# Scaling half of a gate table on ScalarE, and 38 instead of 30 products worked out ahead

## The chip, the cores and the metric

The kernel runs on one core of a Trainium2 chip. The metric is the device time of one execution in microseconds (us), and of several executions the median. The engines are TensorE (PE in the rows; its weight loads are PEld), VectorE (DVE), ScalarE (ACT), GpSimd (POOL, which here issues the gathers of table rows) and SyncE (SP, which issues the other transfers). Each engine works through its own queue in order.

## The reference

One layer of a hybrid decoder runs for 1024 prompt tokens and 8 sample tokens: three mixers (a state-space scan, a convolution branch, attention to a memory), an output projection with layer norm, and then a layer of experts with a second layer norm. The change lies in the expert layer. Each token picks, in each of 8 heads, 16 of 128 x 128 experts, each named by two numbers i and j:

```
u = jnp.take(u_tab, idx, axis=0)
act = jax.nn.gelu(jnp.einsum('td,thkd->thk', t, u), approximate=False)
v = jnp.take(v_tab, idx, axis=0)
return jnp.einsum('thk,thkd->td', gate * act, v)
```

`u_tab` and `v_tab` (here: the first and the second table) have 16384 rows of 1024 numbers.

## The kernel before, in words

The prompt is worked on in three groups of 256, 384 and 384 tokens. For the first two groups the table rows that the tokens chose are gathered one slot at a time: a row of the first table for each of 128 tokens is one gather (L442) of 128 x 1024 numbers, which VectorE multiplies with the tokens and sums (L455). The rows of the second table are either added up on VectorE (L544, `block_v2`) or, in `block_v`, multiplied on TensorE (L501) with a mostly empty weight tile ("slide"); I call eight of these matmuls, which take four gathered tiles, a strip. The sums of a strip block stand in the accumulators named `va` until VectorE reads them (L522). These rows are not a stage of their own. They are spread over the other work: each call of `product` calls `spread`, which lets a number of rows go, set by `PHASES` and `PACE`, with a low priority.

The third group is worked on in full, with no gathers of its own, by `dense_group`. For each of 128 blocks of experts (all j for one i) it needs

- a product: the first table's block times the 384 tokens, followed by Gelu (`activations`, L1296). Ahead of the dense loop it is made with plain fp32 matmuls (L211); in the loop with operands split into a high and a low part (L189 and L191 split the table, L200 multiplies three combinations);
- its gates: for each token the gate at the places (i, j) that the token chose, 0 elsewhere;
- the second table's block, split by L164 and L176 and multiplied in L1385 into six accumulators.

The gate tables are built first, four tokens at a time, in three blocks of 128 tokens: 96 token groups. For each, VectorE compares the token's i with 0 to 127 (L1315, `oi`, four tokens in one instruction), and compares its j with 0 to 127 and scales by the gate (L1319, `oj`, one instruction per token). TensorE multiplies the two (L1321), which puts a token's gates in one of two accumulator banks named `mm`, and ScalarE evicts the bank (L1325) into a tile that goes to memory as `gd`. `oi` and `oj` are taken from a pool of seven tiles (`E2B`). Between the token groups stand products: the first 6 (`PRE`) stay on the chip; then one after every fourth token group (`STEP`) until 30 (`EARLY`) are done, whose results go to memory as `ad`. At the start of each block `route` works out the choices of 128 tokens on VectorE (L343 to L419).

Then the dense loop runs over c from 0 to 127. Iteration c takes product c+6 from `ad` while c+6 is under `EARLY` (and lets rows go at the rates of `PACE[-2]`, 1.0 and 1.0 a call), and computes it afterwards (2.2 and 2.2). VectorE multiplies it with its gates (L1353); I call this a weighing, and there are 128 of them. `keep_tokens`, which copies the group's tokens out, is called at c = 2 x `EARLY`.

A scheduler sets the order on each engine when the program is built: it may move a product past token groups, and puts the gathered rows where it finds room. So a change of a constant moves instructions far from its line.

Of the kernel before, what the change touches and what calls it, by code (L numbers as in the profile page):

```python
# [13 lines left out]
AF = mybir.ActivationFunctionType  # L14
OP = mybir.AluOpType
# [3 lines left out]
P = 128  # L19
# [23 lines left out]
RIDE = 0  # L43
LATER = 1000000
PRE = 6
EARLY = 30
STEP = 4
VLAG = 6
TLAG = 10
E2B = 7  # L50
# [18 lines left out]
def hybrid_layer(ctx: ExitStack, tc, I, O):  # L69
    nc = tc.nc  # L70
    pe, act, dve, pool, sp = nc.tensor, nc.scalar, nc.vector, nc.gpsimd, nc.sync
# [14 lines left out]
    def blk(n=N, dt=F32):  # L86
        t = blkp.tile([P, NW], dt, name="b")
        return t[:, :n]

    def e2(dt=F32):  # L90
        return ep.tile([P, 512], dt, name="e2", bufs=E2B)
# [5 lines left out]
    def pmm():  # L97
        return psp.tile([P, 512], F32, name="mm", bufs=2)
# [15 lines left out]
    def load(shape, src, dt=F32, name="c"):  # L114
        t = cst.tile(shape, dt, name=name)
        sp.dma_start(t, src)
        return t
# [18 lines left out]
    iot = load([P, P], I["iot"], name="iot")  # L136
# [687 lines left out]
    def keep_tokens(G):  # L824

        for c in range(G.tb):
            for i in range(4):
                pt = psm()
                for f in range(2):
                    pe.transpose(pt[:, f * P:(f + 1) * P], G.rs[2 * i + f][:, c * P:(c + 1) * P], ident)  # L830
                xt = blk(256)
                act.activation(xt, pt[:, 0:256], AF.Copy)  # L832
                sp.dma_start(x1d[G.g][c][:, i * 256:(i + 1) * 256], xt)
# [451 lines left out]
    def dense_group(G):  # L1285
# [6 lines left out]
        def activations(c, xs):  # L1292
            ps = (ptp() if c % 2 == 0 else psm())[:, :nt]
            product(ps, I["peer_ut"][c], xs)
            a = accp.tile([P, NW], F32, name="acc")[:, :nt]
            act.activation(a, ps, AF.Gelu)  # L1296
            return a

        ahead = [activations(c, G.rs) for c in range(PRE)]
        ad = drp.tile([P, EARLY, nt], F32, name="ad")  # L1300
        early = PRE
        TG = 4
        for c in range(TB):
            ij = blk(2 * P).rearrange("p (k t s) -> p k t s", k=2, t=1)
            route(P, 1, 8, *([x[:, c:c + 1] for x in t] for t in G.top), None, G.gate[:, c:c + 1],
                  [ij[:, 0], ij[:, 1]])
            pt = pmm()
            for k, src in enumerate((ij[:, 0, 0], ij[:, 1, 0], G.gate[:, c])):
                pe.transpose(pt[:, k * P:(k + 1) * P], src, ident)
            tr = blk().rearrange("p (k t) -> p k t", k=3)  # L1310
            act.activation(tr, pt[:, 0:384].rearrange("p (k t) -> p k t", k=3), AF.Copy)
            for t in range(0, P, TG):
                tt = c * P + t
                oi, oj = (e2().rearrange("p (t i) -> p t i", t=TG) for _ in range(2))
                dve.tensor_tensor(oi, tr[:, 0, t:t + TG].unsqueeze(2).to_broadcast([P, TG, P]),  # L1315
                                  iot.unsqueeze(1).to_broadcast([P, TG, P]), op=OP.is_equal)
                pg = pmm()
                for u in range(TG):
                    dve.tensor_scalar(oj[:, u], iot, tr[:, 1, t + u:t + u + 1], tr[:, 2, t + u:t + u + 1],  # L1319
                                      op0=OP.is_equal, op1=OP.mult)  # L1320
                    pe.matmul(pg[:, u * P:(u + 1) * P], oj[:, u], oi[:, u], start=True, stop=True)  # L1321
                o = tt % QT
                if o == 0:
                    gs = xtp.tile([P, P, QT], F32, name="xt")
                act.activation(gs[:, :, o:o + TG].rearrange("p i t -> p t i"),  # L1325
                               pg.rearrange("p (t i) -> p t i", t=TG), AF.Copy)
                if o + TG == QT:
                    sp.dma_start(gd[:, tt // QT], gs)
                if t // TG % STEP == 0 and early < EARLY:
                    sp.dma_start(ad[:, early], activations(early, G.rs))  # L1330
                    early += 1
# [27 lines left out]
        for c in range(P):  # L1359
            if c + PRE < P:  # L1360
                if c == 2 * EARLY:
                    keep_tokens(G)
# [53 lines left out]
    sample_route()  # L1416
    tables[0].append(sample_experts())
    dense_group(G)
    while more():
        due[:] = 8.0, 8.0  # L1420
# [97 lines left out]
```

## Time and profile before

| | |
|---|---|
| median of 3 runs | 4560.6 us (4558.7 to 4568.8) |
| profiled execution | 4556.4 us, span 4554.6 us |
| TensorE busy | 3933.1 us, 86% |
| VectorE busy | 3289.7 us, 72% |
| ScalarE busy | 1751.8 us, 38% |
| GpSimd busy | 1593.4 us, 35% |
| memory traffic | 1199 MB, 263 GB/s in the mean |

A block of the first table (`wr<-in_peer_ut`) is a load of 512 KB. The token groups run from 3160 to 3415 us after the span's start, the dense loop from there to about 4510. TensorE's busy time includes modelled ends of pipelined matmuls, and each fp32 matmul shows as two passes in the rows.

### The profile page before, as it was taken

How to read it: one execution, taken by the hardware profiler on the slowest of the kernel's cores; microseconds unless marked ns; L12 is line 12 of the kernel's file. 1: busy time of each engine (PE TensorE's matmuls, PEld its weight loads, DVE VectorE, ACT ScalarE, POOL GpSimd, SP SyncE). 2: the span in 40 equal slices, each digit the busy share in tenths (PEclk: the TensorE clock that was granted, in tenths of full speed). 3: DMA queues.
4: the chain of work that ended last, by engine and by line, in shares of the span. 5: the costliest groups of instructions: out<-in, count | busy, mean ns of one | idle time of the engine just before them, and what ended most of it. 6: DMA issues, size and time to landing. Idle time of an engine off the chain costs nothing. (4 is left out here: it accounts for less than half of the span.)

```text
span 4554.6 us, 58299 instructions
## 1 busy us (share of the span) xinstructions
PE 3933.1 (86%) x19901; PEld 3047.6 (67%) x19901; DVE 3289.7 (72%) x7235; ACT 1751.8 (38%) x3696; POOL 1593.4 (35%) x1316
## 2 busy tenths in 40 slices
PE   8998899688898788975888888888996999889996
PEld 8888788567675455553665665445664788778895
DVE  4458835869698546675766796458996899888876
ACT  5475525346432204342362332113562333333333
POOL 0000000123333554413444536534322566556631
PEclk9999999899899998987999999999997999999998
DMA  5435555556677898835878879978879999999985
GB/s 176 149 124 171 180 164 169 202 205 226 220 241 245 302 343 311 291 139 178 282 282 321 304 260 337 341 236 282 305 283 312 359 382 393 343 317 304 389 280 188
DMA packets 410043, 1199.42 MB, mean 263 GB/s; under 512 B 42465, under 2 KB 111713, under 8 KB 407569
## 3 DMA queue, kind: packets, MB, share of 16 engines
q0 software_dynamic: 186880, 679.56, 42.2%
q1 hardware_dynamic: 222864, 516.13, 32.8%
q8 instruction: 157, 2.57, 0.2%
q14 instruction: 142, 1.16, 0.1%
HBM read 1141.59 MB, written 53.93 MB: 262 GB/s over the span
## 5 line engine op out<-in xcount | busy, mean ns | idle before, releaser
L442 POOL DMA_INDIRECT uv<-in_peer_u,idx x640 | 759.0, 1186 | 1831.9 <-DVE idx L422 852.1
L200 PE MATMUL mm<-xt,wh 128*128 128x384 f32 (+1 forms) x4224 | 1045.5, 333 | 37.5 <-ACT b L923 23.9
L455 DVE SCALAR_TENSOR_TENSOR uv<-uv,x 128x1024 f32<-128x1024 f32 x640 | 775.7, 1220 | 395.0 <-DMA uv<-in_peer_u,idx 347.1
L200 PEld LDWEIGHTS mm<-xt,wh 128*128 128x128 f32 x4224 | 745.3, 193 | 100.3 <-issue 33.1
L211 PE MATMUL mm<-b,wr 128*128 128x256 f32 (+2 forms) x2304 | 724.9, 467 | 60.9 <-ACT b L739 34.1
L200 PE MATMUL mm<-xt,wl 128*128 128x384 f32 (+1 forms) x2112 | 692.0, 328 | 37.7 <-DVE wl L191 37.5
L189 ACT ACTIVATE wh<-wr 128x1024 fp32r<-128x1024 f32 x362 | 382.9, 1058 | 864.4 <-PE mm L200 327.0
L442 POOL DMA_INDIRECT uv<-in_peer_v,ixt x384 | 427.6, 1113 | 688.1 <-PE va L501 205.5
L211 PEld LDWEIGHTS mm<-b,wr 128*128 128x128 f32 x2304 | 438.4, 196 | 310.3 <-issue 45.4
L191 DVE TENSOR_TENSOR wl<-wr,wh 128x1024 fp32r<-128x1024 f32 x362 | 441.9, 1221 | 247.1 <-ACT wh L189 229.6
L442 POOL DMA_INDIRECT uv<-in_peer_v,idx x256 | 348.2, 1360 | 345.0 <-DVE uv L544 194.2
L200 PEld LDWEIGHTS mm<-xt,wl 128*128 128x128 f32 x2112 | 406.9, 193 | 57.6 <-DVE wl L191 43.4
L678 DVE SCALAR_TENSOR_TENSOR b<-raw,cc,b 128x384 f32<-128x384 f32 (+1 forms) x720 | 408.7, 569 | 9.9 <-ACT b L676 3.4
L544 DVE SCALAR_TENSOR_TENSOR uv<-uv,av 128x1024 f32<-128x1024 f32 (+1 forms) x269 | 343.5, 1280 | 12.9 <-DMA uv<-in_peer_v,idx 9.9
L501 PE MATMUL va<-uv,slide 128*32 128x512 f32 x1536 | 228.2, 714 | 133.3 <-DMA uv<-in_peer_v,ixt 133.3
L501 PEld LDWEIGHTS va<-uv,slide 128*32 128x32 f32 x1536 | 45.0, 120 | 244.4 <-DMA uv<-in_peer_v,ixt 148.6
L200 PE MATMUL st<-b,wh 128*128 128x384 f32 x784 | 205.7, 344 | 0.5 <-ACT b L832 0.5
L200 PE MATMUL tp<-b,wh 128*128 128x384 f32 x784 | 204.5, 342 | 0.0
L164 ACT ACTIVATE b<-acc 128x384 fp32r<-128x384 f32 x128 | 66.8, 525 | 348.4 <-PE va L1385 261.7
L176 DVE TENSOR_TENSOR wl<-e,wh 128x512 fp32r<-128x512 f32 x256 | 165.1, 684 | 24.2 <-ACT wh L164 22.1
L1385 PE MATMUL mm<-wh,b 128*128 128x512 f32 x512 | 165.2, 404 | 13.7 <-ACT b L164 10.1
L1385 PE MATMUL va<-wh,b 128*128 128x512 f32 x512 | 164.5, 403 | 10.9 <-DVE uv L522 10.9
(409 smaller groups left out, 6382.8 us busy)
## 6 DMA issues: line engine op xcount, KB each, us to landing
wr<-in_win SPq DMA_DIRECT2D x264, 512.0 KB
wr<-in_peer_ut SPq DMA_DIRECT2D x128, 512.0 KB
e<-in_peer_v SPq DMA_DIRECT2D x256, 256.0 KB
wr<-in_wso SPq DMA_DIRECT2D x48, 512.0 KB
wr<-in_wq SPq DMA_DIRECT2D x48, 512.0 KB
gd<-xt SPq DMA_DIRECT2D x16, 1536.0 KB
xt<-gd SPq DMA_DIRECT2D x16, 1536.0 KB
wr<-in_wmo SPq DMA_DIRECT2D x24, 512.0 KB
```

What stands on the lines that cost most here:

```text
L164: act.activation(hi, src, AF.Copy)
L176: dve.tensor_tensor(l, src, f32(h), op=OP.subtract)
L189: act.activation(wh, wr, AF.Copy)
L191: dve.tensor_tensor(wl, wr, f32(wh), op=OP.subtract)
L200: pe.matmul(ps, a[:, k], b[k0 + k], start=(i == 0), stop=(i == n - 1))
L211: pe.matmul(ps, w[:, k], xs[k], start=(k == 0), stop=(k == 7))
L442: pool.indirect_dma_start(out=dst, out_offset=None, in_=table, in_offset=bass.IndirectOffsetOnAxis(ap=idx_col, axis=0))
L455: dve.scalar_tensor_tensor(u, u, 1.0, x1, op0=OP.mult, op1=OP.mult, accum_out=av[:, s:s + 1])
L501: before = pe.matmul(va[dh][32 * j:32 * j + 32], w[:, j, 31 - m:63 - m], vs[j][:, dh * 512:dh * 512 + 512], start=(m == 0), stop=(m == 31) ...
L544: dve.scalar_tensor_tensor(acc, v, av[:, s:s + 1], acc, op0=OP.mult, op1=OP.add)
L678: dve.scalar_tensor_tensor(cv, raw[:, i:i + nt], col(C_FW, j * TAPS + i), cv, op0=OP.mult, op1=OP.add)
L1385: pe.matmul(outs[2 * tbk + dh], a[:, ts], v[:, dh * 512:dh * 512 + 512], start=(c == 0 and i == 0), stop=(c == P - 1 and i == 2))
```

## The change

For two of the four tokens of a group VectorE now compares j with 0 to 127 in one instruction, without scaling, and ScalarE multiplies each token's 128 columns by its gate in place. The other two tokens are compared and scaled by VectorE as before. `EARLY` goes from 30 to 38 and `STEP` from 4 to 3. Through `EARLY` the first 32 instead of 24 iterations of the dense loop take their product from memory, and `keep_tokens` is called at c = 76 instead of 60.

```diff
-EARLY = 30
-STEP = 4
+EARLY = 38
+STEP = 3
...
                 pg = pmm()
+                half = TG // 2
+                dve.tensor_tensor(oj[:, 0:half], tr[:, 1, t:t + half].unsqueeze(2).to_broadcast([P, half, P]),
+                                  iot.unsqueeze(1).to_broadcast([P, half, P]), op=OP.is_equal)
                 for u in range(TG):
-                    dve.tensor_scalar(oj[:, u], iot, tr[:, 1, t + u:t + u + 1], tr[:, 2, t + u:t + u + 1],
-                                      op0=OP.is_equal, op1=OP.mult)
+                    if u < half:
+                        act.activation(oj[:, u], oj[:, u], AF.Copy, scale=tr[:, 2, t + u:t + u + 1])
+                    else:
+                        dve.tensor_scalar(oj[:, u], iot, tr[:, 1, t + u:t + u + 1], tr[:, 2, t + u:t + u + 1],
+                                          op0=OP.is_equal, op1=OP.mult)
                     pe.matmul(pg[:, u * P:(u + 1) * P], oj[:, u], oi[:, u], start=True, stop=True)
```

In the changed kernel the scaling on ScalarE is L1323, the remaining VectorE instruction L1325, the token groups' matmuls L1327, the evictions L1331, the weighings L1359 and the loop's second matmuls L1391.

ScalarE's order in the middle of the second block of tokens before: evictions (`xt<-mm`) in fours, then a product's Gelu (`acc`).

```order
L1325 ACTIVATE xt<-mm 128x4x128 x4
L1296 ACTIVATE acc<-st 128x384
L1325 ACTIVATE xt<-mm 128x4x128 x4
L493 ACTIVATE slide_134<-avt 128x4
L1325 ACTIVATE xt<-mm 128x4x128 x4
L1296 ACTIVATE acc<-tp 128x384
```

The same place now, with the scalings in between (`e_` and a number is one `oj` tile):

```order
L1296 ACTIVATE acc<-tp 128x384
L1331 ACTIVATE xt<-mm 128x4x128
L1323 ACTIVATE e_24844<-e_24844,b 128x128 x2
L1331 ACTIVATE xt<-mm 128x4x128 x2
L1323 ACTIVATE e_24858<-e_24858,b 128x128 x2
L1323 ACTIVATE e_24872<-e_24872,b 128x128 x2
L1296 ACTIVATE acc<-st 128x384
L1331 ACTIVATE xt<-mm 128x4x128
L1323 ACTIVATE e_24907<-e_24907,b 128x128
L1331 ACTIVATE xt<-mm 128x4x128
L1323 ACTIVATE e_24907<-e_24907,b 128x128
L1331 ACTIVATE xt<-mm 128x4x128
```

The scalings of the next two token groups stand ahead of a product's Gelu; that of the third stands behind one eviction (`e_24844`) or has its second half behind two (`e_24907`).

TensorE's order at the end of the token groups before: single matmuls of a product between token groups, a last strip, and then the loop.

```order
L211 MATMUL st<-b,wr 128x384
L1321 MATMUL mm<-e_25599,e_25600 128x128 x4
L211 MATMUL st<-b,wr 128x384
L1321 MATMUL mm<-e_25612,e_25613 128x128 x2
L211 MATMUL st<-b,wr 128x384
L1321 MATMUL mm<-e_25612,e_25613 128x128 x2
L1321 MATMUL mm<-e_25648,e_25649 128x128 x4
L1321 MATMUL mm<-e_25661,e_25662 128x128 x4
L1321 MATMUL mm<-e_25674,e_25675 128x128 x4
L501 MATMUL va<-uv,slide_134 32x512 x8
L1385 MATMUL mm<-wh,b 128x512 x2
```

The same place now:

```order
L211 MATMUL tp<-b,wr 128x384 x8
L1327 MATMUL mm<-e_25856,e_25857 128x128 x4
L1327 MATMUL mm<-e_25871,e_25872 128x128 x4
L1327 MATMUL mm<-e_25886,e_25887 128x128 x4
L211 MATMUL st<-b,wr 128x384 x8
L1327 MATMUL mm<-e_25923,e_25924 128x128 x4
L1327 MATMUL mm<-e_25937,e_25938 128x128 x4
L1327 MATMUL mm<-e_25951,e_25952 128x128 x4
L1327 MATMUL mm<-e_25965,e_25966 128x128 x4
L1391 MATMUL mm<-wh,b 128x512 x2
```

Products stand whole between threes of token groups, and the last strip has moved: the ten strips of the stage now all stand before the last third of the token groups.

VectorE's order just ahead of the first weighing before: rows of the first table (L455) between splittings of the tokens (`b<-b`) and of the second table (`wl`). Two more rows of the first table stand between these and the last token group.

```order
L455 SCALAR_TENSOR_TENSOR uv,av<-uv,x_24769 128x1024
L176 TENSOR_TENSOR b<-b 128x384
L455 SCALAR_TENSOR_TENSOR uv,av<-uv,x_24769 128x1024
L176 TENSOR_TENSOR b<-b 128x384
L176 TENSOR_TENSOR wl<-e_25796,wh 128x512
L176 TENSOR_TENSOR wl<-e_25800,wh 128x512
L455 SCALAR_TENSOR_TENSOR uv,av<-uv,x_24769 128x1024 x4
L1353 TENSOR_TENSOR acc<-acc,xt 128x384 x6
```

The same place now. Two more rows of the first table and three of the second stand between these and the last token group.

```order
L455 SCALAR_TENSOR_TENSOR uv,av<-uv,x_24611 128x1024
L544 SCALAR_TENSOR_TENSOR uv<-uv,av 128x1024
L455 SCALAR_TENSOR_TENSOR uv,av<-uv,x_24611 128x1024
L544 SCALAR_TENSOR_TENSOR uv<-uv,av 128x1024
L176 TENSOR_TENSOR wl<-e_26088,wh 128x512
L176 TENSOR_TENSOR wl<-e_26092,wh 128x512
L544 SCALAR_TENSOR_TENSOR uv<-uv,av 128x1024
L455 SCALAR_TENSOR_TENSOR uv,av<-uv,x_24611 128x1024
L544 SCALAR_TENSOR_TENSOR uv<-uv,av 128x1024
L1359 TENSOR_TENSOR acc<-acc,xt 128x384 x6
```

Rows of the second table (L544) have come to this place, and the splittings of the tokens have moved ahead of it.

## Rows read from the trace of the kernel before

**Rows 1.** The profile's first lines: span, then busy time, share and instructions by engine.
```profile
span 4554.6 us, 58299 instructions
PE 3933.1 (86%) x19901; PEld 3047.6 (67%) x19901; DVE 3289.7 (72%) x7235; ACT 1751.8 (38%) x3696; POOL 1593.4 (35%) x1316
```

**Rows 2.** Windows: token groups by block of 128 tokens, then the passage behind them.
```profile
core 0: us, PE busy (x) PEld busy (x) DVE busy (x) ACT busy (x) POOL busy (x), PEclk, DMA share, GB/s
3160.00:3264.00 104.00, 94.62 (x485) 61.96 (x484) 93.59 (x308) 52.71 (x51) 38.67 (x30) 0.98 0.80 295
3264.00:3363.00 99.00, 92.08 (x480) 60.56 (x479) 90.45 (x301) 54.32 (x53) 30.90 (x26) 0.98 0.77 285
3363.00:3415.00 52.00, 50.43 (x329) 39.57 (x327) 52.00 (x162) 45.22 (x37) 5.35 (x5) 1.00 0.81 315
3415.00:3441.00 26.00, 5.12 (x21) 1.73 (x20) 18.02 (x35) 7.49 (x15) 7.67 (x7) 0.60 1.01 351
```

**Rows 3.** Groups of instructions, 3160 to 3415: line, count | busy us, mean ns | idle before.
```profile
L1325 ACT ACTIVATE xt<-mm 128x512 f32<-128x512 f32 x95 | 132.6, 1467 | 15.7 <-PE mm L1321 13.3 <-PE st L211 0.7 <-DMA gd<-xt 0.3
L1319 DVE TENSOR_SCALAR e<-iot,b 128x128 f32<-128x128 f32 x384 | 107.0, 346 | 6.9 <-PE mm L1321 6.9
L1321 PE MATMUL mm<-e,e 128*128 128x128 f32 x768 | 103.9, 281 | 10.7 <-ACT xt L1325 7.9 <-issue 1.3 <-DVE e L1319 0.4
L211 PE MATMUL st<-b,wr 128*128 128x384 f32 x192 | 69.2, 490 | 0.0
```

**Rows 4.** Chain of waits in the first and the last block: start us, us, what.
```profile
3178.43 5.16 PE tp L211 x16
3183.60 0.91 PE mm L1321 x8
...
3184.53 2.73 ACT xt L1325 x2
...
3187.30 1.16 PE mm L1321 x8
3188.46 1.85 PE va L501 x16
3190.32 5.36 PE st L211 x16
...
3386.71 0.65 PE tp L211 x2
3387.36 0.89 PE mm L1321 x8
```

**Rows 5.** Groups by form, whole span: nearest rows to the new operations.
```profile
L1074 ACT ACTIVATE sb<-sb,s_db 128x128 f32<-128x128 f32 x128 | 41.4, 391 | 41.9 <-DMA sb<-in_sstate 29.8 <-DVE b L678 5.1 <-DVE acc L732 5.0
L349 DVE TENSOR_TENSOR b<-b 128x256 f32<-128x256 f32 x16 | 5.5, 419 | 6.3 <-ACT b L331 6.3
```

**Rows 6.** Timeline of TensorE behind the token groups: start us, us, what [idle before].
```profile
3425.93 3.64 PE L501 MATMUL va<-uv,slide 128*32 128x512 f32 x16 [10.77 <-DMA uv<-in_peer_v,ixt]
3439.68 1.22 PE L1385 MATMUL mm<-wh,b 128*128 128x512 f32 x2 [10.11 <-ACT b L164]
...
3458.38 1.30 PE L1385 MATMUL va<-wh,b 128*128 128x512 f32 x2 [10.86 <-DVE uv L522]
```

**Rows 7.** Windows of the weighings (L1353) in the dense loop: their count in brackets.
```profile
core 0: us, DVE busy (x), PEclk, DMA share, GB/s
3441.40:3471.90 30.50, 3.33 (x7) 0.73 0.80 273
3471.90:3559.50 87.60, 8.91 (x16) 0.93 0.95 328
3597.80:3889.80 292.00, 17.85 (x32) 0.96 1.01 385
3889.80:4286.20 396.40, 22.15 (x40) 0.96 1.00 333
4319.80:4486.50 166.70, 11.03 (x20) 1.00 0.83 278
```

**Rows 8.** Window behind the last weighing, rows of the second table (L544) alone.
```profile
4486.00:4554.00 68.00, 8.97 (x7) 0.74 0.43 147
```

## The prediction

> **What bounds the kernel now.** I read the table of busy times first [rows 1]: TensorE is busy for 86% of the span and VectorE for 72%, so neither fills it, and the change has to be read in its own stages. The windows by stage come next [rows 2]. The gate-table stage lasts 255 us in three thirds of 104, 99 and 52, one for each block of 128 tokens. In all three VectorE is busy for 236.0 us and TensorE for 237.1; both are nearly full. In the last third VectorE is busy for 52.0 of 52.0: 32 groups of four tokens, 1.63 us each, set the pace.
>
> The list of groups [rows 3] and the chain of waits [rows 4] say how the two share the stage. One first-table product costs TensorE 5.16 us (16 passes; 5.36 with a strip ahead of it). Four token groups take 0.91, then two evictions by ScalarE of 1.36 each, then 1.16: 4.8 us, of which only 4 x 0.89 = 3.56 is multiplying. The rest, 1.3 us, is TensorE waiting for one of two accumulator banks. In the last third there is no such loss: two passes of a product (0.65) stand between the token groups (0.89), and ScalarE keeps up.
>
> Then comes a passage [rows 2, 6] of 26 us in which TensorE is busy for 5. It waits 10.77 us for the gathered rows of the last strip, 10.11 for the first weighed product, and 10.86, some iterations into the loop, for VectorE to read that strip's accumulator. Last is the dense loop, which I time by its weighings, one for each of 128 products [rows 7]: 5.5 us each while the products come from memory (87.6/16), 9.1 once they are computed and both kinds of expert rows run beside them (292.0/32, memory at a share of 1.01), 9.9 in the stretch behind it (396.4/40; it holds the samples' rows, the copying out of tokens and a change of block), and 8.3 at the end (166.7/20, granted clock 1.00), where TensorE alone sets it.
>
> **The change part by part.** *Comparing and scaling.* VectorE loses two of four compare-and-scale instructions, 107.0/384 = 0.28 us each [rows 3], and gets one comparison of 128x256, 0.42 by the nearest row [rows 5]; that is 0.14 us less per token group, or 0.2 where neighbours overlap, 13 to 20 us over 96 groups. ScalarE gets 192 scalings. The same form, 128x128 with a scale from a column, takes 0.39 us alone and 41.4/128 = 0.32 in a row [rows 5], so 62 us. ScalarE is busy for 152 of 255 us now [rows 2]; it has the room.
>
> The Trainium skill, "ScalarE: Activation LUTs", section "Rules for kernel authors", puts multiplications on VectorE and not on ScalarE; in "What ACT_TABLE_LOAD costs" it gives 186 ns plus 93 for a column operand plus 0.833 ns per element, of which 93 overlap, an estimate of 0.29 us for 128 elements. The row agrees within a tenth. By the page's figure the waits worked out below would be some 2 us shorter, which decides nothing.
>
> What matters is where the scalings stand. ScalarE works in order, and the piece of its order in the section on the change shows that the scalings of the third token group stand behind the eviction of the first (evict, scale, scale, evict, evict) or even behind the second (evict, scale, evict, scale; evict, evict, scale, scale). TensorE can't start that third group before. With one eviction ahead a group of three takes 0.91 + 1.36 + 0.32 + 1.16 = 3.75 us, 1.1 over its 3 x 0.89; with two ahead 0.91 + 2.73 + 0.32 + 1.1 = 5.1, 2.4 over. I count some 12 of the first kind in the new order, 15 of the second and 5 short ones: 13 + 36 + 2, about 50 us of waiting.
>
> *Eight more products.* TensorE's order has 23 products between the first and the last token group before, 31 now, and they stand whole, three token groups apart, in the last third too, where they were spread. TensorE's work in the stage now: 23 x 5.16 + 96 x 0.89 + 9 strips x 1.85 = 221 us; 34 of the 255 are idle, of which the four-group chains explain 16 x 1.3 = 20. After: 31 x 5.16 + 85 + 10 x 1.85 = 264 us (the tenth strip is the one that stood behind the stage). With idle time as it is now the stage would take 298, +43; with 50 us of waits and the other 14 left as they are 328, +73. Below, the stage can't shrink under what VectorE needs: 236 - 16, and into the stage come, by VectorE's order, 18 more rows of the first table (41 for 23) and 11 of the second at 1.25 us or so (1.28 in [rows 8]) and the end of the strip block, about 6: 262 us, or with the 19 us by which the stage is now over VectorE's time 281, +26. I take +58, midway between unchanged waits and all of those I count, since a scaling that finds ScalarE free costs nothing.
>
> *The passage.* TensorE's order now has all strips ahead of the last token group, two thirds into the stage, so the 10.77 us go. But the gates still have to be written, read back and weighed, and VectorE has 12 expert rows ahead of the first weighing where it had 8, less eight splittings of 128x384 that moved ahead. Of 26 us I take nothing off; -8 to +8, as the rows land (memory was at a share of 1.01 there [rows 2]).
>
> *The loop.* Counting rows between weighings in VectorE's order, the same classes come back with other lengths. Before, from the eighth weighing to the last: 4 with the strip's wait (28.8 of the first window's 30.5 us; its three others come at once behind the first five), 16 early (87.6), 4 mixed (38.3), 32 with both kinds of rows (292.0), 40 of the stretch behind (396.4), 4 and 20 at the end (33.6, 166.7): 1043 us [rows 7]; the pieces of 4 are the gaps between its windows. After: 28 early x 5.48 = 153, 4 mixed 38, 32 with both kinds 292, 20 of the stretch behind, which keep its one-time costs (396.4 - 40 x 9.13 = 31): 183 + 31 = 214, 4 at 34, and 32 at the end x 8.33 = 267: 998. That is -46, of which 7 is the 10.86 us wait. If the one-time costs find cover, -60; if the added early iterations run no better than the first four (7.2 us), -33.
>
> *Behind the loop.* Ten rows of the second table instead of seven stand behind the last weighing: 3 x 1.28 [rows 8] = +4, or 0 where they hide under the layer norm.
>
> The sum: +58 + 0 - 46 + 4 = +16 us. The profiled execution took 4556.4 us, which is 4.2 under the median of the runs, 4560.6; the step added to either gives 4572 or 4577. I forecast 4576 us, slower.
>
> **Rivals.** *VectorE stays the bound.* It is full in the last third and 0.90 and 0.91 busy in the first two [rows 2]. If ScalarE scales during the 5.16 us that TensorE spends on a product, as it does for the first two groups of three, the waits don't grow and VectorE's 16 us of relief, less the rows that move in, are what counts: the stage grows by 26 to 30, say 28, and the sum is 28 - 46 + 4 = -14: 4547 us. Against it: the order puts the third group's scaling behind an eviction that itself waits for TensorE. It decides if TensorE's waits for ScalarE stay under about 20 us.
>
> *The stage pays exactly for its work.* Idle time stays at 34 us: +43 - 46 + 4 = +1, 4561 us, no change. For it: ScalarE has 100 us to spare.
>
> *Memory collides with the strips.* Into a stage at a share of 0.77 to 0.81 [rows 2] come eight tables of 0.5 MB, their results and 29 more gathers; TensorE stands in order behind strips that wait for gathers (10.77 us once already [rows 6]). With all the waits I count (+73) and another 5 us for strips: 4560.6 + 73 + 5 - 46 + 4 = 4597 us.
>
> **How the numbers follow.** The forecast has a chance of 0.45, the collision 0.13, the even stage 0.22, VectorE as the bound 0.20. About 0.2%, 9 us, is what a measurement of this kernel can tell from no change. Faster by more: 0.20; within: 0.22; slower: 0.58. The low end is the stage at VectorE's bound with the loop halfway to its best, 26 - 53 + 4 = -23, about 4540; the high end is the collision and 5 us more, 4602. The forecast's own range is 4570 to 4590 (the stage +52 to +66).
>
> **What would show it.** The stage from the first to the last token group at about 313 us, not 278 or 298; TensorE's waits for ScalarE on the token groups at 30 us or more; the wait for the last strip and for its accumulator gone; 32 weighings at 5.5 us and a loop shorter by 46 us. A stage under 290 us, or a loop shorter by more than 60, would make the forecast wrong; so would a passage that shrinks by more than 10.

## The result, and the profile after

The changed kernel takes 4594.0 us (median of 6 runs, 4586.7 to 4601.8), the kernel before 4562.6 beside it: a ratio of 1.0068, with an interval of 1.0049 to 1.0088, or 31 us more. It is slower, as forecast, and 18 us slower than the 4576 that I had named; the time lies within the whole range (4540 to 4602) and outside the 4570 to 4590 of the forecast itself. The profiled execution took 4601.1 us, 45 more than that of before; 10 of these lie ahead of the gate-table stage, where both kernels have the same work and the start wanders from execution to execution (last section).

The first lines of its profile (span; then busy time, share and instructions by engine) answer to [rows 1]:

```profile
span 4599.4 us, 58346 instructions
PE 3933.7 (86%) x19837; PEld 3033.6 (66%) x19837; DVE 3266.6 (71%) x7131; ACT 1784.5 (39%) x3880; POOL 1577.9 (34%) x1316
```

TensorE is busy for 3933.7 us where it was 3933.1. Eight products are made in 16 passes each ahead of the loop and no longer in 24 matmuls in it (64 instructions fewer), at the same busy time in the sum, so the added time is time in which TensorE stands idle. The windows show where. First the kernel before, in four parts: the gate-table stage, the passage to the sixth weighing, the dense loop, and what stands behind it (us, then busy time of PE, PEld, DVE, ACT and POOL with counts, granted clock, memory share, GB/s).

```profile
3161.00:3415.00 254.00, 236.13 (x1288) 161.52 (x1286) 235.20 (x768) 152.11 (x138) 74.17 (x61) 0.99 0.79 295
...
3441.00:4486.00 1045.00, 964.84 (x4559) 845.46 (x4559) 870.39 (x1137) 355.29 (x594) 560.15 (x405) 0.96 0.96 338
4486.00:4554.00 68.00, 30.70 (x125) 22.39 (x123) 40.91 (x44) 28.51 (x47) 0.00 (x0) 0.74 0.43 147
sum 1393.00, PE 1236.79 PEld 1031.10 DVE 1164.52 ACT 543.41 POOL 642.00; mean PE 309.20 PEld 257.78 DVE 291.13 ACT 135.85 POOL 160.50
```

Then the changed kernel, in the same parts:

```profile
3171.00:3499.00 328.00, 284.97 (x1430) 189.36 (x1428) 269.16 (x737) 203.34 (x351) 118.10 (x97) 0.96 0.84 305
3499.00:3534.00 35.00, 1.19 (x5) 0.86 (x4) 16.30 (x23) 5.24 (x8) 12.30 (x12) 0.53 1.03 384
3534.00:4525.00 991.00, 921.01 (x4368) 803.29 (x4367) 809.26 (x1069) 339.01 (x570) 494.28 (x361) 0.97 0.94 328
4525.00:4599.00 74.00, 30.70 (x124) 22.36 (x122) 44.90 (x47) 28.50 (x46) 3.73 (x3) 0.71 0.45 157
sum 1428.00, PE 1237.87 PEld 1015.87 DVE 1139.62 ACT 576.09 POOL 628.41; mean PE 309.47 PEld 253.97 DVE 284.90 ACT 144.02 POOL 157.10
```

From the stage's start on, 1393 us became 1428. TensorE's busy time moved and did not grow: +48.8 in the stage, -43.8 in the loop, 1236.8 and 1237.9 in the sum. Its idle time is the length of a part less its busy time: 17.9 to 43.0 us in the stage, 20.9 to 33.8 in the passage, 80.2 to 70.0 in the loop, 37.3 to 43.3 behind it. That is +25, +13, -10 and +6, or +34 us. This sum of idle time is the measure for the experiments below. It is a rough one: TensorE's busy time in the four parts goes from 1226 to 1249 us over the kernels of the table, so that some 10 us in a single profile say little.

What TensorE waits for in the stage is in the groups by form, 3171 to 3499 (busy us, mean ns | idle time before, by what ended it), to be held against [rows 3]:

```profile
L1327 PE MATMUL mm<-e,e 128*128 128x128 f32 x768 | 101.8, 282 | 26.5 <-ACT xt L1331 15.5 <-ACT e L1323 9.7 <-issue 1.3
L501 PE MATMUL va<-uv,slide 128*32 128x512 f32 x160 | 25.0, 753 | 16.5 <-DMA uv<-in_peer_v,ixt 16.5
L1323 ACT ACTIVATE e<-e,b 128x128 f32<-128x128 f32 x191 | 63.2, 396 | 9.7 <-DVE e L1319 9.6
L1319 DVE TENSOR_TENSOR e<-b,iot 128x256 f32<-128x256 f32 x95 | 39.8, 419 | 30.0 <-PE mm L1327 28.9 <-ACT xt L1331 1.1
L455 DVE SCALAR_TENSOR_TENSOR uv<-uv,x 128x1024 f32<-128x1024 f32 x43 | 51.9, 1219 | 21.3 <-DMA uv<-in_peer_u,idx 21.2
```

The rows of the kernel before that [rows 3] leaves out, 3161 to 3415:

```profile
L455 DVE SCALAR_TENSOR_TENSOR uv<-uv,x 128x1024 f32<-128x1024 f32 x23 | 27.9, 1212 | 7.4 <-DMA uv<-in_peer_u,idx 7.4
L501 PE MATMUL va<-uv,slide 128*32 128x512 f32 x144 | 19.6, 665 | 7.2 <-DMA uv<-in_peer_v,ixt 7.2
```

On the token groups TensorE waits 15.5 us for evictions and 9.7 for the new scalings, and another 16.5 for the gathered rows of the strips, which was 7.2 before. With the 10.77 us that the last strip waited in the passage [rows 6] it was 18.0, though: the strips' waits moved into the stage with that strip and did not grow. VectorE, which waited for gathered rows for 7.4 us, waits for 21.2. The prices were as forecast: 63.2 us for 191 scalings (62 expected), 0.419 for the comparison (0.42).

The release by "ACT e" isn't always ScalarE's doing. The longest such wait, in the timeline of the changed kernel at the start of the second block (start us, us, engine, line; in brackets the idle time and its releaser):

```profile
3288.52 1.23 DVE L455 SCALAR_TENSOR_TENSOR uv<-uv,x 128x1024 f32<-128x1024 f32 x1 [4.14 <-DMA uv<-in_peer_u,idx]
...
3290.83 0.42 DVE L1319 TENSOR_TENSOR e<-b,iot 128x256 f32<-128x256 f32 x1
...
3291.34 0.69 ACT L1323 ACTIVATE e<-e,b 128x128 f32<-128x128 f32 x2 [7.16 <-DVE e L1319]
...
3291.80 2.08 PE L1327 MATMUL mm<-e,e 128*128 128x128 f32 x8 [7.51 <-ACT e L1323]
```

Read upwards: TensorE waits 7.51 us for a scaling; ScalarE had waited 7.16 for the comparison; and VectorE, in order, stood at an expert row whose gather had not landed. Of the 9.7 us put down to scalings 7.5 stand behind that gather and the row that waited for it.

The passage in the chain of waits of the changed kernel (start us, us, what):

```profile
3500.76 12.89 DMA gd<-xt
...
3513.66 18.18 DMA xt<-gd
...
3531.86 1.18 DVE acc L1359 x3
```

The last 1.5 MB of gates are written and the first 1.5 MB of the loop's read back in 31.1 us, at a memory share of 1.03. Before, the chain through the passage went over a strip's rows and an expert row:

```profile
3417.38 8.50 DMA uv<-in_peer_v,ixt
...
3429.82 7.42 DMA uv<-in_peer_u,idx
```

These waits are gone from the chain, and the writing and reading back now decides. For the loop, windows of the weighings alone answer to [rows 7], for the same three classes:

```profile
3536.00:3658.00 122.00, 13.52 (x25) 0.93 0.98 342
3716.00:4005.00 289.00, 17.64 (x32) 0.99 1.01 386
4257.00:4525.00 268.00, 17.94 (x33) 1.00 0.83 281
```

Between the weighings lie 24 intervals of 5.1 us, 32 of 9.0 and 32 of 8.4 (a window with both of its ends on a weighing counts one more): the classes of before, with other lengths. The wait for the strip's accumulator, 10.86 us some iterations into the loop [rows 6], is gone: the multiplications that stood behind it (`va<-wh`) wait for nothing over the whole span, and the loop's first (`mm<-wh`) wait for the passage:

```profile
L1391 PE MATMUL mm<-wh,b 128*128 128x512 f32 x512 | 163.1, 400 | 34.5 <-ACT b L164 33.8
L1391 PE MATMUL va<-wh,b 128*128 128x512 f32 x512 | 160.5, 394 | 0.0
```

Behind the last weighing stand ten rows of the second table (L544), to be held against [rows 8]:

```profile
4525.00:4599.00 74.00, 12.83 (x10) 0.71 0.45 157
```

### The profile page after: what moved, and what is told of

The parts are those of the page before. It is cut to its first block, busy times and chain, and to the rows that moved or that the text cites. A ratio compares the mean times of both kernels' runs of the same rounds, so it can differ in the third digit from the quotient of the medians.

```text
span 4599.4 us, 58346 instructions
## 1 busy us (share of the span) xinstructions
PE 3933.7 (86%) x19837; PEld 3033.6 (66%) x19837; DVE 3266.6 (71%) x7131; ACT 1784.5 (39%) x3880; POOL 1577.9 (34%) x1316
## 5 line engine op out<-in xcount | busy, mean ns | idle before, releaser
L442 POOL DMA_INDIRECT uv<-in_peer_u,idx x640 | 748.1, 1169 | 1853.7 <-DVE idx L422 856.9
L455 DVE SCALAR_TENSOR_TENSOR uv<-uv,x 128x1024 f32<-128x1024 f32 x640 | 775.5, 1221 | 408.7 <-DMA uv<-in_peer_u,idx 356.0
L191 DVE TENSOR_TENSOR wl<-wr,wh 128x1024 fp32r<-128x1024 f32 x354 | 432.2, 1222 | 267.6 <-ACT wh L189 260.9
L544 DVE SCALAR_TENSOR_TENSOR uv<-uv,av 128x1024 f32<-128x1024 f32 (+1 forms) x269 | 343.7, 1280 | 20.1 <-DMA uv<-in_peer_v,idx 13.4
L1391 PE MATMUL mm<-wh,b 128*128 128x512 f32 x512 | 163.1, 400 | 34.5 <-ACT b L164 33.8
L200 PE MATMUL tp<-b,wh 128*128 128x384 f32 x720 | 189.1, 345 | 0.0
L200 PE MATMUL st<-b,wh 128*128 128x384 f32 x720 | 187.1, 341 | 0.5 <-ACT b L832 0.5
L164 ACT ACTIVATE wh<-e 128x512 fp32r<-128x512 f32 x256 | 148.8, 625 | 51.5 <-DMA e<-in_peer_v 29.3
```

The lines of the kernel that those rows point to most:

```text
L164: act.activation(hi, src, AF.Copy)
L191: dve.tensor_tensor(wl, wr, f32(wh), op=OP.subtract)
L200: pe.matmul(ps, a[:, k], b[k0 + k], start=(i == 0), stop=(i == n - 1))
L442: pool.indirect_dma_start(out=dst, out_offset=None, in_=table, in_offset=bass.IndirectOffsetOnAxis(ap=idx_col, axis=0))
L455: dve.scalar_tensor_tensor(u, u, 1.0, x1, op0=OP.mult, op1=OP.mult, accum_out=av[:, s:s + 1])
L544: dve.scalar_tensor_tensor(acc, v, av[:, s:s + 1], acc, op0=OP.mult, op1=OP.add)
```

## The experiments

Three theories. A, the one behind the forecast: the order on ScalarE, scalings and evictions in each other's way. B: only the work of the eight products, which moves from the loop into the stage. C: expert rows and their gathers, of which more came into the stage (by VectorE's order 47 of the first table and 20 of the second up to the first weighing, 31 and 0 before: each product lets rows go, and the eight bring theirs along), collide with strips and read-backs. Part names and lines are those of the changed kernel. All results in one table: us of the four parts in the profiled execution, TensorE's idle time in them together, and the ratio of the runs to the kernel before.

| kernel | stage | passage | loop | behind | idle | ratio (95%) |
|---|---|---|---|---|---|---|
| before | 254 | 26 | 1045 | 68 | 156 | |
| changed | 328 | 35 | 991 | 74 | 190 | 1.0068 (1.0049 to 1.0088) |
| scalings only | 277 | 19 | 1027 | 69 | 162 | 1.0039 (1.0020 to 1.0058) |
| the same again | 279 | 20 | 1037 | 68 | 166 | 1.0043 (1.0022 to 1.0063) |
| 38 products only | 335 | 33 | 995 | 75 | 195 | 1.0108 (1.0086 to 1.0130) |
| changed, four banks | 315 | 34 | 989 | 75 | 187 | 1.0073 (1.0048 to 1.0097) |
| before, four banks | 252 | 25 | 1041 | 69 | 155 | 1.0003 (0.9989 to 1.0017) |
| changed, fewer rows in the stage | 299 | 18 | 1025 | 121 | 218 | 1.0159 (1.0135 to 1.0183) |
| changed, four banks, scalings first | 317 | 35 | 983 | 74 | 180 | 1.0060 (1.0036 to 1.0084) |
| the two above together | 279 | 19 | 1025 | 120 | 207 | 1.0140 (1.0114 to 1.0166) |
| scalings only, four banks, first | 271 | 23 | 1035 | 70 | 164 | 1.0008 (0.9988 to 1.0027) |
| together, rows hidden later | 284 | 19 | 1024 | 72 | 156 | 1.0041 (1.0023 to 1.0059) |
| scalings only, rows later | 261 | 19 | 1078 | 77 | 186 | 1.0100 (1.0073 to 1.0127) |
| before, rows later | 253 | 21 | 1074 | 75 | 182 | 1.0071 (1.0045 to 1.0096) |

**One part of the change at a time.** The scalings with thirty products:

```diff
-EARLY = 38
-STEP = 3
+EARLY = 30
+STEP = 4
```

> The scaling on ScalarE alone, with 30 products worked out ahead, one after every fourth token group, as before. Theory A (the order on ScalarE: scalings stand between evictions and TensorE waits for them): the token-group stage, 255 us before, keeps its 221 us of TensorE work, VectorE is relieved by 13 to 20 us, but TensorE's waits for ScalarE grow by about as much; 4555 to 4575 us, and TensorE's waits for the scaling (L1323) show at 10 us or more. Theory B (the cost is only the work of the eight products that were moved): VectorE was the stage's bound, so the relief comes through, stage about 240 us, 4545 to 4552 us. Theory C (the rows that came into the stage collide with the strips): no rows come in here, so as theory B.

And the eight products with VectorE scaling all four tokens:

```diff
-                half = TG // 2
-                dve.tensor_tensor(oj[:, 0:half], tr[:, 1, t:t + half].unsqueeze(2).to_broadcast([P, half, P]),
-                                  iot.unsqueeze(1).to_broadcast([P, half, P]), op=OP.is_equal)
...
-                    if u < half:
-                        act.activation(oj[:, u], oj[:, u], AF.Copy, scale=tr[:, 2, t + u:t + u + 1])
-                    else:
-                        dve.tensor_scalar(oj[:, u], iot, tr[:, 1, t + u:t + u + 1], tr[:, 2, t + u:t + u + 1],
-                                          op0=OP.is_equal, op1=OP.mult)
+                    dve.tensor_scalar(oj[:, u], iot, tr[:, 1, t + u:t + u + 1], tr[:, 2, t + u:t + u + 1],
+                                      op0=OP.is_equal, op1=OP.mult)
```

> 38 products ahead, one after every third token group, with all four tokens compared and scaled by VectorE as before. Theory A: without scalings between the evictions a group of three costs TensorE 0.91 + 1.36 + 1.16 us; stage about 300 us instead of 328 in the changed kernel, bounded by VectorE (236 + 29 rows x 1.25 + 6 + 19), loop as in the changed kernel; about 4565 to 4575 us. Theory B: the eight products cost the same with or without the scaling; 4588 to 4600 us, as the changed kernel. Theory C: the same rows come into the stage (44 and 16 instead of 47 and 20 of the two tables up to the first weighing), VectorE has more to do; 4590 us or more.

Scalings alone cost 0.39%, products alone 1.08%, both 0.68%. They don't add up: with thirty products the scalings lose some 0.4%, with 38 they win back 0.4% of what the products cost. The loss with thirty is in A's range, but A's sign is missing: TensorE's waits for the scalings on the token groups are 2.2 us (10 or more were to show), those for evictions 13.1 for 7.9. Its four parts sum to 1392 us for 1393 before, so that its profile doesn't show where the 0.4% lie. The stage with the products alone, its two main waits (columns as above):

```profile
L1321 PE MATMUL mm<-e,e 128*128 128x128 f32 x767 | 101.1, 281 | 23.0 <-ACT xt L1325 19.1 <-DVE e L1319 2.2 <-issue 1.5
L501 PE MATMUL va<-uv,slide 128*32 128x512 f32 x160 | 25.3, 763 | 26.6 <-DMA uv<-in_peer_v,ixt 26.6
```

Without one scaling on ScalarE the stage is 335 us long, and TensorE waits for evictions (19.1) and strips (26.6). So the scalings aren't what makes the stage long; A can't be the whole. The Trainium skill ("ScalarE: Activation LUTs", "Rules for kernel authors") would keep multiplications on VectorE: with thirty products the runs agree (1.0039), with 38 they don't (1.0068 against 1.0108).

**Four banks.** Of changed and before alike, so that an eviction holds up no token group:

```diff
-                pg = pmm()
+                pg = pmm() if t // TG % 2 else pss()
```

> The changed kernel with four accumulator banks for the token groups instead of two (the two banks of the name ss take turns with mm). The waits of TensorE for a free bank (15.5 us of its own, 22.2 in its weight loads) go. Theory A: the third group of three still waits for its scaling, which stands behind one or two evictions; 0 to 12 us faster than the changed kernel, and waits for L1323 grow. If the banks alone were the cause: 25 to 35 us faster, stage at 295 us. Theory C: waits for gathers (16.5 us of TensorE, 21.2 of VectorE) stay; 5 to 15 us faster.

> The kernel before with four accumulator banks instead of two. The four-group chains cost TensorE 20 us of waits, but VectorE is the bound of that stage (236 of 255 us): 0 to 5 us faster, stage 250 to 255 us. If TensorE's waits for a bank set the stage: 12 to 20 us faster.

Neither ratio moves: 1.0073 for 1.0068, and 1.0003. The waits do. In the changed kernel with four banks, 3164 to 3479:

```profile
L1327 PE MATMUL ss<-e,e 128*128 128x128 f32 x384 | 52.4, 280 | 11.6 <-ACT e L1323 11.6
L1327 PE MATMUL mm<-e,e 128*128 128x128 f32 x384 | 52.1, 278 | 4.5 <-ACT e L1323 4.5
...
L501 PE MATMUL va<-uv,slide 128*32 128x512 f32 x160 | 24.3, 733 | 21.6 <-DMA uv<-in_peer_v,ixt 21.6
```

The 15.5 us for evictions are gone, but 16.1 are put down to scalings (9.7 before) and 21.6 to strips (16.5). The bank was only what came last. The stage is 13 us shorter in this profile, but that is the kernel's fastest run (4578.6 us, the median is 4587.8), and the runs don't show it.

**Fewer rows in the stage (C), scalings first (A), and both.** The pace at which the planner spreads expert rows, set lower as the stage begins:

```diff
         TG = 4
+        pace[0] = 0.5, 2.0
```

> The kernel after the change, with the planner's pace of expert rows set lower from the start of the gate-table stage on: by VectorE's order 17 rows of the first table and none of the second stand between the first token group and the first weighing, for 47 and 20 in the changed kernel; they come later, in the loop. Scalings, products and banks are as in the changed kernel. Theory C (rows and gathers that came into the stage collide with the strips): the 16.5 us that TensorE waits there for gathers and part of VectorE's 21.2 us of waits for gathers go, the stage shrinks from 328 us to 300 or below, the passage stays at some 33, and the rows, 30 x 1.28 = 38 us of VectorE's time, come back in the loop where they lie beside TensorE: 20 us or more less than the changed kernel, ratio to the kernel before about 1.002. Theory A (the order on ScalarE: scalings between evictions): the waits for ScalarE, 25 us on matrix multiplications, stay, the stage stays above 315, and the loop gets longer by what moves: within 10 us of the changed kernel. Theory B (the work of the eight products alone): the stage stays at 31 x 5.16 + 85 and idle time, no change against the changed kernel.

Scalings given priority on ScalarE, with four banks:

```diff
-                pg = pmm()
+                pg = pmm() if t // TG % 2 else pss()
...
-                        act.activation(oj[:, u], oj[:, u], AF.Copy, scale=tr[:, 2, t + u:t + u + 1])
+                        with tc.high_priority(LATER):
+                            act.activation(oj[:, u], oj[:, u], AF.Copy, scale=tr[:, 2, t + u:t + u + 1])
```

> The kernel after the change with four accumulator banks for the token groups, and with the two scalings put ahead on ScalarE: in its order they now stand ahead of evictions that are due at the same time, mostly evict, scale, scale, and no longer evict, scale, evict, scale. Rows, products and pace are as in the changed kernel. Theory A: TensorE's waits for the scalings (9.7 us with two banks, 16.0 with four banks alone) and for evictions (15.5 us with two banks) both go, the stage falls from 328 us to about 300, and the kernel is 20 us or more faster than the changed one: ratio to the kernel before near 1.002. Theory C: the waits move on to the strips' gathers as they did with four banks alone (16.5 to 21.6 us), and the stage stays at 310 or more: ratio 1.005 to 1.008. Theory B: no change against four banks alone, ratio 1.007.

Then both edits in one kernel:

> The kernel after the change with both edits: scalings ahead on ScalarE and four banks, and the lower pace of rows in the stage. If A and C each hold in part, the stage falls to 31 x 5.16 + 96 x 0.89 + 10 x 1.85 = 264 us and some 15 of idle time, about 280, with the loop some 10 to 20 us longer by the rows that move into it: about 1425 - 48 + 15 = 1392 us from the start of the stage for 1425 after the change and 1390 before, a ratio of about 1.000 to the kernel before. If only B holds, the ratio stays at 1.006 to 1.008, since the eight products cost their own time wherever scalings and rows stand.

In the stage and the passage both theories hold, C for more. Fewer rows: 328 to 299 and 35 to 18. TensorE's waits in that stage, 3176 to 3475:

```profile
L1328 PE MATMUL mm<-e,e 128*128 128x128 f32 x766 | 100.8, 281 | 22.0 <-ACT xt L1332 17.1 <-ACT e L1324 4.9
L501 PE MATMUL va<-uv,slide 128*32 128x512 f32 x160 | 19.2, 598 | 0.0
```

The strips' 16.5 us are gone; of the 25.2 for ScalarE 22.0 stay, as A said. Scalings first: 328 to 317, of which four banks alone give 13, so that the priority shows nothing of its own. Both: 279 and 19, where 280 was expected, so that banks and order, worth 11 us with the rows in the stage, are worth 20 without them. Fewer rows also mean 48 us less of work for VectorE (269.2 to 221.1 busy); what that gives and what the gathers give was not tried apart. In the kernel with both edits and a later pace in the loop (below; 3167 to 3451) the strips wait for nothing either, and the passage's two transfers take 13.4 us where they took 31.1:

```profile
L501 PE MATMUL va<-uv,slide 128*32 128x512 f32 x160 | 20.4, 629 | 0.0
```

```profile
3453.73 6.13 DMA gd<-xt
...
3459.87 7.25 DMA xt<-gd
```

But the whole got slower, 1.0159 and 1.0140, against every expectation: I had the rows come back under cover of the loop. The loop grew by 34 us, and 47 came behind it, where 43 rows stand for ten: the loop's own pace of second-table rows was too low to bring them in.

The scalings alone, with the same two edits on ScalarE and the banks:

> The kernel before the change with the scalings alone (thirty first-table products ahead, one in four token groups, as before), four banks, and the scalings put ahead on ScalarE. With scalings alone the ratio was 1.0039, with 13.1 us of waits of TensorE for evictions and 16.6 for the strips' gathers. Theory A: without the waits for ScalarE VectorE's relief is left, 13 to 20 us in the last third: faster than the kernel before, ratio 0.996 to 0.999. Theory C: the strips' gathers, which scalings alone brought into the stage, still cost their 16.6 us: ratio 1.002 to 1.004.

The 0.4% that scalings alone cost are gone: 1.0008, between the two expectations. A's edit took the loss away, but no gain from VectorE's relief is left over: TensorE still waits 21.5 us for strips, as C said, though before it was 18.0 in the stage and the passage together. Banks and order were not tried apart here.

**The same rows, hidden later.** The loop's pace raised as well, so that 10 or 11 rows stand behind the last weighing:

```diff
-PACE = (1.5, 2.0), (1.0, 1.0), (2.2, 2.2)
+PACE = (1.5, 2.0), (1.0, 1.0), (2.2, 3.0)
```

> The changed kernel with scalings ahead, four banks and few rows in the stage, as in the last run with both, and a higher pace of second-table rows in the loop (2.9 to 3.0 an iteration for 2.2), so that by VectorE's order 11 rows stand behind the last weighing for 43. There the stage had shrunk to 279 us, but the loop took 1026 and the stretch behind it 117. Theory C with cover: the last 24 iterations, which TensorE alone sets at 8.3 us, hide the 32 rows: behind the loop 72 us, the loop unchanged, from the start of the stage 279 + 19 + 1026 + 72 = 1396 us for 1425 in the changed kernel and 1390 before: ratio about 1.001. Rival: the rows have no cover in the loop (32 x 1.28 = 41 us of VectorE and 32 gathers): the loop grows by what the end loses, ratio 1.010 or more.

The kernel falls from 1.0140 to 1.0041, between the two expectations, and its profile does what C with cover expected: 284 + 19 + 1024 + 72 = 1399 us. The 120 us behind the loop are 72 again, and the loop paid nothing for it. The last 24 iterations of this kernel, and then of the changed one:

```profile
4294.00:4494.00 200.00, 199.80 (x1003) 180.60 (x1002) 188.29 (x210) 73.79 (x121) 118.92 (x90) 1.00 1.00 377
```

```profile
4324.00:4525.00 201.00, 201.00 (x1009) 181.85 (x1008) 146.22 (x174) 73.40 (x121) 70.00 (x52) 1.00 0.82 277
```

VectorE goes from 146 to 188 of 200 us and the memory share from 0.82 to 1.00, and TensorE stays full. Against the kernel with scalings first and the old pace, the stage is 33 us shorter and the passage 16, and the loop 41 longer: the rows moved into the stage had cost about as much there as they saved in the loop. That the runs say +0.41% while this profile has the idle time of before (156) is in part the execution: it took 4568.5 us, the median of the kernel's runs is 4579.0.

Nearly the same pace (0.5 in the stage, 2.9 in the loop, for ten rows behind it) for the scalings alone, and for the kernel before with nothing else changed:

> The scalings alone (thirty products ahead), four banks, scalings put ahead on ScalarE, few rows of the expert tables in the stage (13 of the first table by VectorE's order for 31) and the higher pace of second-table rows in the loop. Theory C: the 21.5 us that TensorE waits for the strips' gathers go and VectorE has 18 x 1.28 = 23 us less to do in the stage, so it falls from 271 to about 240 us (work of TensorE: 23 x 5.16 + 85 + 19 = 223), the passage to 19; the loop takes 1040 to 1050 and the end 72: about 1376 us for 1390 before, ratio 0.997. If the rows have no cover later: 1395 or more, ratio 1.001 or above.

> The kernel before the change with the pace of rows alone changed as in the run with scalings (few in the stage, more in the loop). It tells what the rows are worth without any part of the change. If VectorE sets the stage, it falls by up to 23 us and with it the strips' waits, as with the scalings: ratio 0.997; then the scalings are worth nothing even with the rows gone. If VectorE still sets the last third at 1.63 us per token group, as in the kernel before, it falls by 10 to 15 us only, and the run with scalings is 5 to 10 us faster than this one: ratio about 1.000 here.

The gains expected failed: 1.0100 and 1.0071. For the scalings the rival came true, rows without cover (1.001 or above). In the kernel before, eighteen rows fewer up to the first weighing (ten of them in the stage) leave the stage at 253 us and take 5 off the passage, and the loop grows by 29. What TensorE waits for in the middle of the loop (engine, line, waited for: us, times, longest us), of this kernel from 3659 to 4316 (64 iterations) and of the kernel before from 3598 to 4286 (72):

```profile
PE st L200 <- DVE wl L191: 34.0, 13, 8.0
PE tp L200 <- DVE wl L191: 31.8, 16, 4.6
```

```profile
PE st L200 <- DVE wl L191: 23.7, 8, 8.2
PE tp L200 <- DVE wl L191: 13.2, 7, 3.2
```

L191 splits the next block of the first table on VectorE; it comes later, 65.8 us of waits for 36.9. Why is not shown: where both kinds of rows run, VectorE's order has about 34 rows to eight weighings in both kernels, 19 or 20 of them of the second table instead of 16 to 18. With thirty products the rows are nearly free in the stage and dear in the loop.

Four kernels with four banks and scalings first lie side by side here. At the old pace the eight products cost 0.5% (1.0008 to 1.0060), at the later one they win 0.6% (1.0100 to 1.0041). So whether the eight products pay hangs on where the rows stand, and C's gain comes only with 38.

Last, the scalings alone once more:

> The kernel with the scalings alone once more. Its first profile had 1.2 us less than the kernel before from the start of the stage on, and 19 us more ahead of it, where the two kernels have the same instructions, yet its runs were 18 us slower than before. If the part ahead only wanders from execution to execution: another start of the stage in this profile (3161 to 3185 us), and a ratio between 1.000 and 1.004. If the scalings make the part ahead longer in every execution: the start again near 3180 us, and the ratio again 1.004.

The ratio comes again, 1.0043, while the pieces of the profile trade places: the stage starts at 3163 us instead of 3180, the loop takes 1037 instead of 1027. The loss is real, and the part ahead only wanders. The stage and the passage come again within 2 us, the start and the loop within 10 to 20, and single profiles are to be read accordingly.

No version beats the kernel before. The nearest are it with four banks (1.0003) and the scalings with theirs (1.0008).

## Why the prediction was right, and where it was not

*The direction, and what bounds the kernel.* Right. TensorE stands at 86%, its busy time is the same, and the stage grew by more than the loop shrank.

*Comparing and scaling.* The prices held, and the waits for ScalarE were there. I counted 50 us of them if all were paid and took about half; TensorE waited 25.2 us on the token groups (30 or more were to show), of which 7.5 stood behind a gather; for evictions it had been 7.9 [rows 3]. The two figures are not one measure: the same way of counting gave 20 us for the kernel before, where the row has 7.9, and 34 us of idle time where the windows have 17.9 [rows 2]. What relieving ScalarE is worth was overrated: banks and order made the stage 11 us shorter and the whole kernel no faster (1.0060 for 1.0068).

*Eight more products.* This is the step that failed in size: "I take +58, midway between unchanged waits and all of those I count". It measured +74, at the upper end. TensorE's busy time accounts for 48.8 (I had 43) and idle time for 25. The 328 us are what my sum with all the waits gave, but that is in part luck: 16.5 us of the idle time are the strips', and without one scaling the stage is longer still (335 us). Of the 29 us that fewer rows save, 16.5 are these waits; the waits for ScalarE fall by 3 only. I had put the rows at VectorE's time only, as the lower bound; as late data, ahead of comparisons in VectorE's order and of strips in TensorE's, they stood in the rival with the collision, at 0.13. Its 4597 us came nearest to the time, with the mechanism half right: it too had all the waits for ScalarE in its sum.

*The passage.* "Of 26 us I take nothing off; -8 to +8" measured +9. The strip's wait went, as forecast. What was late next was the read-back of the gates, against gathers at a memory share of 1.03; with the rows gone the passage is 18 to 19 us.

*The loop.* -46 forecast, -54 measured. The three classes came back, 9.0 and 8.4 us for the later two (9.13 and 8.33 taken), and 5.1 instead of 5.48 for the early one, which is 24 x 0.4 = 10 us and accounts for the difference. What the classes hid is how much of the gain was the rows': with these and fourteen more back in the loop (17 up to the first weighing, where the kernel before has 31) it is 1024 us, 21 less than before. An estimate from my own prices agrees: the eight products as such give back 8 x (8.33 - 5.48) = 23 us in iterations and cost 8 x 5.16 = 41 in the stage. The rest of the loop's gain was rows that had moved; the rest of the stage's loss was rows and waits.

*Behind the loop.* +4 forecast, +6 measured, with the ten rows.

*The other rivals.* VectorE as the bound would have needed waits for ScalarE under 20 us: without the 7.5 of the gather they were 17.7, yet the stage was 47 us over the 281 of that case, since VectorE itself waited for gathers (21.2) and for TensorE's release of buffers (28.9). The even stage, 298 us, is what fewer rows make (299), but then the rows come due elsewhere.

What stays open: why the version with rows hidden later still measures 0.41% when its profile from the stage on is 6 us longer than that of before. The profiled execution took 4568.5 us, 10.5 under the kernel's median; which part is longer in the others, this one profile doesn't tell. Open too is where the scalings alone lose their 0.4%, and whether the rows in the stage cost by VectorE's time or by their late gathers.

## What to carry to other kernels

Where a change moves work of the busiest engine between stages, take its busy time over all of them first: if the sum stays, only idle time counts, and each stage's length less the engine's busy time says where it went. What a stage loses when planned filler work moves in is seen only after that filler is moved out again and hidden elsewhere; without the second step the experiment measures the filler's new place. So try old and new at both places of the filler: the eight products lost at one and won at the other. And a wait that names a cheap engine is to be followed up its own wait: here a scaling of 0.4 us stood for a gather.

## What the runs showed that was not expected

The stage's start, behind the same instructions on TensorE, wandered between 3150 and 3180 us over the profiled executions, and the same kernel had it at 3163 and 3180. Writing and reading back 1.5 MB of gates took 12.9 and 18.2 us with row gathers beside it (memory share 1.03) and 6.1 and 7.3 without (0.92). VectorE at 188 of 200 us and memory at a share of 1.00 left TensorE full at 199.8, which I would have thought too tight.
